# The context's first chunk in full fp32 between the products of the lead, in both FFNs of a trunk layer

## The chip, the cores and the metric

The kernel runs on one core of a Trainium2 chip. The metric is the device time of one execution in microseconds, the lower the better. TensorE has two clock levels here, 1.2 and 2.4 GHz; the profile gives the granted clock as a share of the higher one.

## The reference

One layer of a flow-matching backbone for 128 context tokens and 1024 latent tokens (1152 rows of 1024 features), everything in fp32:

```python
def _swiglu(h, w1, w2):
    a, b = jnp.split(h @ w1, 2, axis=-1)
    return (jax.nn.silu(a) * b) @ w2

def _layer(x, mod, lw, rope, kv_ctx):
    f1 = _swiglu(_modulate(x, sh1, sc1), lw['ffn1_w1'], lw['ffn1_w2'])
    x = _layer_norm(ALPHA * x + 0.5 * g1 * f1, ...)
    mix, k, v = _mixer(_modulate(x, sh2, sc2), lw, rope, kv_ctx)
    x = _layer_norm(ALPHA * x + g2 * mix, ...)
    f2 = _swiglu(_modulate(x, sh3, sc3), lw['ffn2_w1'], lw['ffn2_w2'])
    x = _layer_norm(ALPHA * x + 0.5 * g3 * f2, ...)
```

`w1` of an FFN is 1024 x 5632 and `w2` 2816 x 1024. The modulation is x * (1 + scale) + shift per feature, with one pair of vectors for the context and one for the latents.

## The kernel before

**Products.** A matrix product in near-fp32 accuracy is made of three fp32r matmuls (`mm3`, L130 to L132). Each operand is split into a high part, rounded by ScalarE (an ACTIVATE with Copy, L107), and the rest, subtracted on VectorE (L108). TensorE also takes plain fp32 operands: the trace then shows two records for one matmul. The transposes (L135), the modulation's products (L224) and the context's attention scores (L1348) are such plain fp32 work.

**An FFN.** The latent rows are 1024, in two halves of 512. The first weight matrix is worked through in 22 pairs of blocks of 128 columns. A pair is computed by a scheme with seven products in place of eight, on the halves of rows, features and columns: `A11`, `A12`, `S1`, `S2`, `S4`, `S3`, `A22`, in this order. Their moving operands, the two halves of x and sums and differences of them, are split once per FFN; the weights, sums of them too, are split for each pair. The first four pairs are the **lead** (`lead`): they run product by product, all four pairs through one product before the next, so that the operands can be made meanwhile. The text calls A11 the lead's first product, A12 its second, S1 its third and S2 its fourth. `up` then runs the other 18 pairs one behind another, and `down` the second matrix.

In the lead, `first_sum` loads two blocks of a pair's weights and subtracts them (L711) into the third product's weight; for the fourth, L738 subtracts once more. `second` adds the second product's bank into SBUF (L667), which frees the bank. There are eight PSUM banks of 128 x 512; four hold `Y` of the four pairs for most of the lead.

In the first FFN, x comes from the inputs already transposed, and the modulation vectors themselves are computed during the lead (`mod_head`). In the second (`begun`), the first product runs at the end of the mixer (`lead_first`), and the pieces of x are loaded from DRAM, transposed on TensorE and modulated on ScalarE (L402, `piece_dram`): first-half pieces (`piece(0, k)`) and second-half pieces (`piece(1, k)`). `S1` needs the second half only.

**The context.** Its 128 rows go through both FFNs on their own (`ctx_ffn`), in six chunks of columns: five of 512 per half of w1, one of 256. A chunk takes eight weight tiles of 128 x 1024 (`w1c`, 512 KB), each with two output banks; then silu, product, transposes, and the rows of `w2`. `ctx_ffn` is a generator that yields after each piece of work, 155 in all. `tick(n)` advances it n times, and the calls of `tick` in `lead` and `up_prod` set where its work stands in the program. Before, the first FFN gives it to the side queue behind the lead; the second FFN advances it 18 times in the lead ahead of the third product's weights (that is the first chunk) and 5 times in the last product.

**Buffers and queues.** Weight tiles from DRAM go through a ring of five buffers (`raw`, 128 x 1024), loaded on SP's queue. Rings `pc`, `tmp`, `b2`, `xm`, `ts` hold pieces, sums and operands. The program is traced in this order and then planned by the framework with modelled times (`schedule_with_timeline_sim=True`): an instruction traced earlier has priority, and one whose operands and buffers are there may go ahead of it. The engines then run the planned order strictly, waiting on semaphores.

Of the kernel before, what the change touches and what calls it, by code (L numbers as in the profile page):

```python
# [32 lines left out]
P = 128  # L33
# [21 lines left out]
class Layer:  # L55
# [364 lines left out]
    def piece_dram(self, n, kc):  # L420
        r = self.raw(self.x2_d[1 + n][:, :, kc * P : (kc + 1) * P], 512)
        b = self.bank()
        for t in range(4):
            self.transpose(b[:, t * P : (t + 1) * P], r[:, t * P : (t + 1) * P])
        m = self.piece_place(n, kc)
        self.modulated(m, b, 2, LAT, kc)
        return m
# [6 lines left out]
    def open_early(self, right):  # L434
# [7 lines left out]
        def gen():  # L442
            for kc in range(KC):
                self.first_operand(self.piece_dram, kc)
                yield
            yield from self.ctx_x_dram()
# [29 lines left out]
    def ctx_operands(self):  # L476
        place = self.xm if "xm" in self.pools else self.pc
        self.xc = [(place(F32R), place(F32R)) for _ in range(2)]

    def ctx_x(self, x, i, kcs):  # L480
        for kc in kcs:
            m = self.pc()[:, :P]
            self.modulated(m, x[kc], i, CTX, kc)
            ks = slice(kc % 4 * P, (kc % 4 + 1) * P)
            self.split(self.xc[kc // 4][0][:, ks], self.xc[kc // 4][1][:, ks], m)

    def ctx_x_dram(self):
        self.ctx_operands()
        for h in range(2):
            m = self.raw(self.x2_d[0][:, h * 512 : (h + 1) * 512], 512)  # L490
            b = self.bank()
            js = [slice(j * P, (j + 1) * P) for j in range(4)]
            for j in js:
                self.transpose(b[:, j], m[:, j])
            for k, j in enumerate(js):
                self.modulated(m[:, j], b[:, j], 2, CTX, 4 * h + k)
            self.split(self.xc[h][0], self.xc[h][1], m)
            yield

    def ctx_up(self, b, w, kc, n):  # L500
        hi, lo = self.wide(self.raw(w, 2 * n), 2 * n)
        ks = slice(kc % 4 * P, (kc % 4 + 1) * P)
# [6 lines left out]
    def ctx_ffn(self, i, x, w1c, w1t, w2):  # L509
        nc = self.nc  # L510
        if x:
            self.ctx_operands()
            x()
        yield
        acc = None
        for c in range(6):
            n = 256 if c == 5 else 512
            banks = [self.bank(), self.bank()]
            for kc in range(KC):
                yield from self.ctx_up(banks, w1t[kc] if c == 5 else w1c[c, kc], kc, n)  # L520
            h = self.tmp() if c == 0 and "xm" in self.pools else self.pc()
# [58 lines left out]
    def up_pair(self, m, w1, h_d):  # L580
# [17 lines left out]
        self.up_prod(Z, "A12", (hi[:, 512:], lo[:, 512:]), True, 1 + self.spare * (m < 15))  # L598
# [12 lines left out]
        self.up_prod(Y, "S2", [halves(w)[1] for w in t12], False, 1 + self.spare)  # L611
# [38 lines left out]
    def lead(self, w1, h_d, piece, make, Y=None):  # L650
# [44 lines left out]
        else:  # L695
# [6 lines left out]
            self.tick(18)  # L702
# [10 lines left out]
        if begun:  # L713
            for p in R:
                first_sum(p)
            W = [self.wide(T[p], 512) for p in R]
            self.first = [piece(0, k) for k in R]
# [12 lines left out]
        else:  # L730
            for p in R:
                first_sum(p)
                X.append(self.bank())
                prod(X[p], "S1", self.wide(T[p], 512), True)
# [15 lines left out]
        for p in R:  # L750
# [11 lines left out]
            if begun and p == 0:  # L762
# [223 lines left out]
    def ffn(self, i, head, res_of, dst, order, half, beside=None, begun=None):  # L986
# [3 lines left out]
        with ExitStack() as st:  # L990
# [13 lines left out]
            if begun:  # L1004
                self.add_side(context)
            self.lead(a["w1_" + s], h_d, piece, make, Y)
            self.mods = mods
            if not begun:
                self.add_side(context)
# [12 lines left out]
    def head_input(self):  # L1022
        nc, a = self.nc, self.a

        def ctx_x():
            for q in range(4):
                x = self.pc()
                nc.sync.dma_start(x[:, :256], a["x_c"][q])
                self.ctx_x({q: x[:, :P], q + 4: x[:, P:256]}, 0, (q, q + 4))
# [17 lines left out]
        return self.piece_input, make, ctx_x, mods()  # L1047

    def head_dram(self):
        return self.piece_dram, lambda kc: None, None, self.mod_part(8)  # L1050
# [536 lines left out]
def _layout(inputs):  # L1587
# [32 lines left out]
    for i, w in enumerate(WINDOWS):  # L1620
# [6 lines left out]
        "x_c": con(x[:P].T.reshape(2, 4, P, P).transpose(1, 2, 0, 3)).reshape(4, P, 256),  # L1627
# [56 lines left out]
```

## Time and profile before

| | |
|---|---|
| time, median of 3 runs | 2495.24 us (2494.67 to 2498.43) |
| the profiled execution's own time | 2495.49 us |
| its span, first to last instruction | 2493.7 us |
| mean granted TensorE clock | 0.995 |
| busy: TensorE, VectorE, ScalarE | 2452.3, 1830.6, 1214.5 us |

A matmul's record has the time from its start to its modelled end. Matmuls overlap, so the pace is read from the starts, and a bracket behind a row gives the idle time before it and what ended it. PE is TensorE, DVE is VectorE, ACT is ScalarE, POOL is GpSimd, SP issues DMAs; PEq, SPq and so on are their queues.

### The profile page before, as it was taken

How to read it: one execution, taken by the hardware profiler on the slowest of the kernel's cores; microseconds unless marked ns; L12 is line 12 of the kernel's file. 1: busy time of each engine (PE TensorE's matmuls, PEld its weight loads, DVE VectorE, ACT ScalarE, POOL GpSimd, SP SyncE). 2: the span in 40 equal slices, each digit the busy share in tenths (PEclk: the TensorE clock that was granted, in tenths of full speed). 3: DMA queues.
4: the chain of work that ended last, by engine and by line, in shares of the span. 5: the costliest groups of instructions: out<-in, count | busy, mean ns of one | idle time of the engine just before them, and what ended most of it. 6: DMA issues, size and time to landing. Idle time of an engine off the chain costs nothing.

```text
span 2493.7 us, 34226 instructions
## 1 busy us (share of the span) xinstructions
PE 2452.3 (98%) x12297; PEld 2115.0 (85%) x12297; DVE 1830.6 (73%) x2817; ACT 1214.5 (49%) x2094; POOL 463.4 (19%) x691
## 2 busy tenths in 40 slices
PE   8999999999999999999999999999899999999998
PEld 4788888888889989889999999998688888887887
DVE  6877778877678556566888886876877666676877
ACT  5544444444445343434778773435744344444442
POOL 0000011110022212232567640110000001111002
PEclk9999999999999999999999999999999999999999
DMA  7455566778686555534100035665754445558773
GB/s 292 144 167 188 182 224 230 244 259 326 213 276 218 184 180 189 188 136 163 42 1 2 1 110 187 237 215 185 223 173 164 150 173 195 205 197 320 269 267 121
DMA packets 167554, 463.75 MB, mean 186 GB/s; under 512 B 18900, under 2 KB 37636, under 8 KB 167384
## 3 DMA queue, kind: packets, MB, share of 16 engines
q1 hardware_dynamic: 140952, 373.79, 44.7%
q0 software_dynamic: 23696, 86.32, 9.3%
q8 instruction: 97, 1.59, 0.3%
q10 hardware_dynamic: 2736, 1.44, 0.2%
q14 instruction: 73, 0.60, 0.1%
HBM read 390.42 MB, written 71.07 MB: 185 GB/s over the span
## 4 chain that ended last, share of the span: by engine, by line
PE 84%; DVE 6%; issue 4%; DMA 3%; ACT 2%; POOL 1%; SPq 0%; DVEq 0%; POOLq 0%; ACTq 0%
PE w L130 24%; PE w L131 24%; PE w L132 24%; PE w L1060 8%; PE w L135 3%; DVE op L108 1%; DVE x L108 1%; DMA raw<-w 1%; DVE mx L1389 1%; PE w L224 0%; DMA yc<-fc 0%; ACT pr L1397 0%; DMA raw<-w1c 0%; DVE so L108 0%; DMA raw<-x 0%
## 5 line engine op out<-in xcount | busy, mean ns | idle before, releaser
L107 ACT ACTIVATE op<-raw 128x1024 fp32r<-128x1024 f32 (+1 forms) x505 | 483.9, 969 | 517.4 <-PE w L131 263.4
L108 DVE TENSOR_TENSOR op<-raw,op 128x1024 fp32r<-128x1024 f32 (+1 forms) x505 | 558.9, 1116 | 233.1 <-ACT op L107 201.1
L130 PE MATMUL w<-b,op 128*128 128x512 f32 x880 | 343.9, 393 | 7.1 <-ACT b L107 2.9
L131 PE MATMUL w<-b,op 128*128 128x512 f32 x880 | 344.6, 392 | 0.0
L132 PE MATMUL w<-b,op 128*128 128x512 f32 x880 | 339.7, 391 | 0.3 <-DVE op L108 0.3
L130 PE MATMUL w<-x,op 128*128 128x384 f32 x768 | 260.0, 339 | 0.0
L131 PE MATMUL w<-x,op 128*128 128x384 f32 x768 | 258.8, 337 | 0.0
L132 PE MATMUL w<-x,op 128*128 128x384 f32 x768 | 257.7, 337 | 0.0
L131 PE MATMUL w<-op,so 128*128 128x512 f32 (+1 forms) x627 | 242.4, 387 | 2.0 <-DVE op L108 2.0
L132 PE MATMUL w<-op,so 128*128 128x512 f32 (+1 forms) x627 | 241.9, 387 | 0.0
L130 PE MATMUL w<-op,so 128*128 128x512 f32 (+1 forms) x627 | 232.7, 386 | 1.0 <-ACT op L107 0.9
L130 PEld LDWEIGHTS w<-b,op 128*128 128x128 f32 x880 | 165.6, 188 | 42.9 <-ACT b L107 3.4
L562 POOL DMA_DIRECT2D h<-tmp x80 | 43.4, 543 | 851.6 <-DVE tmp L626 426.1
L132 PEld LDWEIGHTS w<-b,op 128*128 128x128 f32 x880 | 165.8, 188 | 35.8 <-DVE op L108 0.8
L131 PEld LDWEIGHTS w<-b,op 128*128 128x128 f32 x880 | 165.8, 188 | 34.8 <-DVE b L108 0.7
L1402 POOL TENSOR_TENSOR pr<-pr,sm 128x384 f32<-128x384 f32 x192 | 156.1, 842 | 95.1 <-DVE sm L1400 71.8
L190 DVE SCALAR_TENSOR_TENSOR junk<-raw,sil 128x1024 bf16<-128x1024 f32 x112 | 135.9, 1224 | 26.0 <-DMA raw<-w_mod 25.6
L107 ACT ACTIVATE so<-sr 128x1024 fp32r<-128x1024 f32 (+1 forms) x84 | 82.7, 986 | 136.1 <-PE w L131 82.7
L131 PEld LDWEIGHTS w<-x,op 128*128 128x128 f32 x768 | 144.1, 188 | 0.3
L130 PEld LDWEIGHTS w<-x,op 128*128 128x128 f32 x768 | 144.1, 188 | 0.4
L132 PEld LDWEIGHTS w<-x,op 128*128 128x128 f32 x768 | 143.9, 188 | 0.0
L131 PEld LDWEIGHTS w<-op,so 128*128 128x128 f32 x627 | 118.2, 189 | 26.8 <-DVE op L108 3.2
(323 smaller groups left out, 5136.6 us busy)
## 6 DMA issues: line engine op xcount, KB each, us to landing
raw<-w SPq DMA_DIRECT2D x240, 256.0 KB, 5.3
raw<-w SPq DMA_DIRECT2D x116, 512.0 KB, 3.9
raw<-w1c SPq DMA_DIRECT2D x80, 512.0 KB, 4.0
sr<-h SPq DMA_DIRECT2D x70, 512.0 KB, 5.7
raw<-w_mod SPq DMA_DIRECT2D x56, 512.0 KB, 4.3
raw<-w_gate SPq DMA_DIRECT2D x48, 512.0 KB, 3.7
h<-tmp POOLq DMA_DIRECT2D x80, 256.0 KB, 3.6
h<-pc POOLq DMA_DIRECT2D x52, 256.0 KB, 4.6
```

The source lines that it names most:

```text
L107: self.nc.scalar.activation(hi, src, AF.Copy)
L108: self.nc.vector.tensor_tensor(lo, src, hi.bitcast(F32), ALU.subtract)
L130: mm(out, lhsT=lh, rhs=rh, start=start, stop=False)
L131: mm(out, lhsT=lh, rhs=rl, start=False, stop=False)
L132: mm(out, lhsT=ll, rhs=rh, start=False, stop=stop)
L135: self.nc.tensor.transpose(out, src, self.ident)
L190: nc.vector.scalar_tensor_tensor(junk, w, 1.0, self.sil[cond], ALU.mult, ALU.mult, accum_out=self.mod[:, cond, b : b + 1],)
L562: self.nc.gpsimd.dma_start(h_d[f // 2][:, 2 * kh + n, f % 2, :], h)
L1060: self.nc.tensor.matmul(acc[h][j], lhsT=lhs[:, part, js], rhs=w[wi][:, h * 512 : (h + 1) * 512], start=f, stop=l)
L1389: nc.vector.tensor_reduce(mx[:, c : c + 1], b[:, :GT], AX.X, ALU.max)
L1402: nc.gpsimd.tensor_tensor(pr[:, c, :], pr[:, c, :], sm[:, 3:4].broadcast_to([P, GT]), ALU.mult)
```

## The change

In both FFNs the context's first chunk is computed with one plain fp32 matmul per weight tile and bank, on modulated rows (`xf`) and weights that are not split. The rows of the first FFN are loaded in two tiles and modulated in place; they are loaded, modulated and split again for the other chunks (`ctx_parts_input`, at the second chunk). Those of the second FFN are modulated at the end of the mixer as before, and split at the second chunk (`ctx_parts_dram`).

The first FFN's context now joins the side queue ahead of the lead, and both leads make the 18 calls behind the third product's weights (loads, sums and splits of all four pairs) and ahead of its matmuls, and the 5 calls in the last product. The calls in `up_prod` of the first FFN are fewer by the same number. In the second FFN the raw loads of the second-half pieces go through POOL's queue into slots of `b2` instead of the ring of five.

```diff
     def piece_dram(self, n, kc):
-        r = self.raw(self.x2_d[1 + n][:, :, kc * P : (kc + 1) * P], 512)
+        src = self.x2_d[1 + n][:, :, kc * P : (kc + 1) * P]
+        if n == 0:
+            r = self.raw(src, 512)
+        else:
+            r = self.pools["b2"].tile([P, 512], F32, tag="b2", name=self.name("xr"), bufs=12)
+            self.nc.gpsimd.dma_start(r.rearrange("p (a b) -> p a b", a=4), src)
...
-            yield from self.ctx_x_dram()
+            yield from self.ctx_whole_dram()
...
-    def ctx_x(self, x, i, kcs):
-        for kc in kcs:
-            m = self.pc()[:, :P]
-            self.modulated(m, x[kc], i, CTX, kc)
-            ks = slice(kc % 4 * P, (kc % 4 + 1) * P)
-            self.split(self.xc[kc // 4][0][:, ks], self.xc[kc // 4][1][:, ks], m)
...
+    def ctx_whole_input(self):
+        self.xf = [self.tmp() for _ in range(2)]
+        for h, x in enumerate(self.xf):
+            self.nc.sync.dma_start(x, self.a["x_c"][h])
+            for k in range(4):
+                js, kc = slice(k * P, (k + 1) * P), 4 * h + k
+                self.modulated(x[:, js], x[:, js], 0, CTX, kc)
+
+    def ctx_parts_input(self):
+        self.xc = [(self.pc(F32R), self.pc(F32R)) for _ in range(2)]
         for h in range(2):
-            m = self.raw(self.x2_d[0][:, h * 512 : (h + 1) * 512], 512)
+            m = self.pc()
+            self.nc.sync.dma_start(m, self.a["x_c"][h])
+            for k in range(4):
+                js = slice(k * P, (k + 1) * P)
+                self.modulated(m[:, js], m[:, js], 0, CTX, 4 * h + k)
+            self.split(self.xc[h][0], self.xc[h][1], m)
+
+    def ctx_whole_dram(self):
+        self.xf = []
+        for h in range(2):
+            r = self.raw(self.x2_d[0][:, h * 512 : (h + 1) * 512], 512)
             b = self.bank()
+            x = self.xm()
+            self.xf.append(x)
             js = [slice(j * P, (j + 1) * P) for j in range(4)]
             for j in js:
-                self.transpose(b[:, j], m[:, j])
+                self.transpose(b[:, j], r[:, j])
             for k, j in enumerate(js):
-                self.modulated(m[:, j], b[:, j], 2, CTX, 4 * h + k)
-            self.split(self.xc[h][0], self.xc[h][1], m)
+                self.modulated(x[:, j], b[:, j], 2, CTX, 4 * h + k)
             yield
 
-    def ctx_up(self, b, w, kc, n):
+    def ctx_parts_dram(self):
+        self.xc = []
+        for x in self.xf:
+            hi, lo = self.xm(F32R), self.pc(F32R)
+            self.split(hi, lo, x)
+            self.xc.append((hi, lo))
+
+    def ctx_up(self, b, w, kc, n, whole):
+        ks = slice(kc % 4 * P, (kc % 4 + 1) * P)
+        if whole:
+            r = self.raw(w, 2 * n)
+            for s in range(2):
+                self.nc.tensor.matmul(
+                    b[s][:, :n], lhsT=self.xf[kc // 4][:, ks], rhs=r[:, s * n : (s + 1) * n],
+                    start=kc == 0, stop=kc == KC - 1,
+                )
+                yield
+            return
         hi, lo = self.wide(self.raw(w, 2 * n), 2 * n)
...
+        whole, parts = x
+        if whole:
+            whole()
         yield
         acc = None
         for c in range(6):
             n = 256 if c == 5 else 512
             banks = [self.bank(), self.bank()]
+            if c == 1:
+                parts()
             for kc in range(KC):
-                yield from self.ctx_up(banks, w1t[kc] if c == 5 else w1c[c, kc], kc, n)
-            h = self.tmp() if c == 0 and "xm" in self.pools else self.pc()
+                yield from self.ctx_up(banks, w1t[kc] if c == 5 else w1c[c, kc], kc, n, c == 0)
+            h = self.tmp() if c == 0 else self.pc()
...
-        self.up_prod(Z, "A12", (hi[:, 512:], lo[:, 512:]), True, 1 + self.spare * (m < 15))
+        self.up_prod(Z, "A12", (hi[:, 512:], lo[:, 512:]), True, 1 + self.spare * (m < 10))
...
-        self.up_prod(Y, "S2", [halves(w)[1] for w in t12], False, 1 + self.spare)
+        self.up_prod(Y, "S2", [halves(w)[1] for w in t12], False)
...
             for p in R:
                 second(p, self.bank(), True)
-            self.tick(18)
...
             W = [self.wide(T[p], 512) for p in R]
+            self.tick(18)
             self.first = [piece(0, k) for k in R]
...
         else:
             for p in R:
                 first_sum(p)
+            W = [self.wide(T[p], 512) for p in R]
+            self.tick(18)
+            for p in R:
                 X.append(self.bank())
-                prod(X[p], "S1", self.wide(T[p], 512), True)
+                prod(X[p], "S1", W[p], True)
                 self.next_operand(p, *S[p])
...
-            if begun and p == 0:
+            if p == 0:
                 self.tick(5)
...
-            if begun:
-                self.add_side(context)
+            self.add_side(context)
             self.lead(a["w1_" + s], h_d, piece, make, Y)
             self.mods = mods
-            if not begun:
-                self.add_side(context)
```

The context's input is laid out as two tiles of 128 x 512 to suit.

## Rows read from the trace of the kernel before

**Rows 1.** The page's busy times: us, share of the span, instructions.
```profile
PE 2452.3 (98%) x12297; PEld 2115.0 (85%) x12297; DVE 1830.6 (73%) x2817; ACT 1214.5 (49%) x2094; POOL 463.4 (19%) x691
```
**Rows 2.** Busy time by stretch: length, engines, granted clock, DMA share, GB/s.
```profile
47.00:72.00 25.00, 19.18 (x70) 13.48 (x68) 24.81 (x49) 19.25 (x35) 0.00 (x0) 0.86 0.27 83
72.00:1757.00 1685.00, 1671.87 (x8865) 1492.49 (x8864) 1247.78 (x2027) 848.31 (x1592) 390.48 (x576) 1.00 0.52 175
1757.00:1800.00 43.00, 35.66 (x176) 26.83 (x175) 31.42 (x45) 28.67 (x43) 0.66 (x2) 1.00 0.71 216
65.00:70.00 5.00, 4.48 (x11) 3.52 (x12) 5.00 (x9) 4.40 (x8) 0.00 (x0) 0.50 0.36 103
```
**Rows 3.** TensorE in order of time, first lead: start, duration, line.
```profile
60.02 0.39 PE L132 MATMUL w<-ax,op 128*128 128x512 f32 x1
...
65.52 0.79 PE L130 MATMUL w<-b,op 128*128 128x512 f32 x1 [2.52 <-DVE tmp L667]
...
70.33 0.40 PE L132 MATMUL w<-b,op 128*128 128x512 f32 x1
```
**Rows 4.** VectorE in order of time, both leads.
```profile
60.56 0.69 DVE L738 TENSOR_TENSOR ts<-raw,ts 128x512 f32<-128x512 f32 x1
...
64.78 2.48 DVE L667 TENSOR_TENSOR tmp<-w,tmp 128x512 f32<-128x512 f32 x4
...
1758.89 1.22 DVE L108 TENSOR_TENSOR op<-raw,op 128x1024 fp32r<-128x1024 f32 x1
```
**Rows 5.** Waits of TensorE, 1757 to 1800: total us, times, longest.
```profile
PE w L135 <- DMA raw<-x: 3.0, 5, 1.5
PE w L130 <- ACT b L107: 2.9, 2, 2.3
PE w L135 <- ACT xp L402: 0.8, 2, 0.6
PE w L132 <- DVE op L108: 0.3, 1, 0.3
```
**Rows 6.** TensorE in order of time: fp32 matmuls and what starts next.
```profile
29.28 3.62 PE L224 MATMUL w<-wm,silt 128*2 128x256 f32 x16
32.83 1.20 PE L130 MATMUL w<-ax,op 128*128 128x512 f32 x4
...
1185.93 1.05 PE L1348 MATMUL w<-kcT,q 128*128 128x128 f32 x8
1186.74 0.42 PE L131 MATMUL w<-x,op 128*128 128x384 f32 x1
```
**Rows 7.** TensorE in order of time: first and last of 26 fp32r matmuls.
```profile
73.08 0.39 PE L130 MATMUL w<-b,op 128*128 128x512 f32 x1
...
78.74 0.39 PE L131 MATMUL w<-b,op 128*128 128x512 f32 x1
```
**Rows 8.** ScalarE's groups by form, 0 to 130: busy us, mean ns.
```profile
L107 ACT ACTIVATE op<-raw 128x1024 fp32r<-128x1024 f32 x5 | 5.2, 1059 | 6.6 <-PE w L131 4.5 <-PE w L132 2.1
...
L402 ACT ACTIVATE pc<-pc,md 128x128 f32<-128x128 f32 x8 | 3.8, 488 | 3.9 <-DMA pc<-x_c 3.9
```
**Rows 9.** Waits of SP's queue, 1757 to 1800.
```profile
SPq L111 <- PE w L135: 15.8, 12, 3.1
```
**Rows 10.** POOL in order of time, second lead.
```profile
1821.66 0.55 POOL L562 DMA_DIRECT2D h<-tmp  x1 [62.39 <-DVE tmp L748]
```
**Rows 11.** DMA of 1766 to 1786: packets, MB, share; size, us to landing.
```profile
q1 hardware_dynamic: 8491, 4.77, 83.1%
...
raw<-x SPq DMA_DIRECT2D x16, 256.0 KB, 3.6
```
**Rows 12.** TensorE in order of time, second lead: chunk, transposes, third product.
```profile
1757.57 0.40 PE L130 MATMUL w<-op,xm 128*128 128x512 f32 x1
...
1775.01 0.63 PE L135 MATMUL w<-ident,raw 128*128 128x128 f32 x4 [0.78 <-DMA raw<-x]
...
1778.73 0.73 PE L130 MATMUL w<-b,op 128*128 128x512 f32 x2 [2.25 <-ACT b L107]
```

More of the change, by code (lines that the diff above doesn't have):

```diff
@@ L473, in last_operands @@
         self.A["A22"].append(self.parted(r, "b2", 12))
-    def ctx_operands(self):
-        place = self.xm if "xm" in self.pools else self.pc
-        self.xc = [(place(F32R), place(F32R)) for _ in range(2)]
-    def ctx_x(self, x, i, kcs):
-        for kc in kcs:
-            m = self.pc()[:, :P]
-            self.modulated(m, x[kc], i, CTX, kc)
-            ks = slice(kc % 4 * P, (kc % 4 + 1) * P)
-            self.split(self.xc[kc // 4][0][:, ks], self.xc[kc // 4][1][:, ks], m)
-    def ctx_x_dram(self):
-        self.ctx_operands()
-        for h in range(2):
-            m = self.raw(self.x2_d[0][:, h * 512 : (h + 1) * 512], 512)
+    def ctx_whole_input(self):
[5 more added lines that the diff above has]
+                self.modulated(x[:, js], x[:, js], 0, CTX, kc)
@@ L501, in ctx_up @@
         hi, lo = self.wide(self.raw(w, 2 * n), 2 * n)
-        ks = slice(kc % 4 * P, (kc % 4 + 1) * P)
         xh, xl = self.xc[kc // 4]
@@ L510, in ctx_ffn @@
         nc = self.nc
-        if x:
-            self.ctx_operands()
-            x()
+        whole, parts = x
+        if whole:
+            whole()
         yield
@@ L1023, in head_input @@
         nc, a = self.nc, self.a
[L1025 to L1029, printed above, removed]
         def mods():
@@ L1045, in make @@
                 self.spread(1, rows[2:])
-        return self.piece_input, make, ctx_x, mods()
+        return self.piece_input, make, (self.ctx_whole_input, self.ctx_parts_input), mods()
     def head_dram(self):
-        return self.piece_dram, lambda kc: None, None, self.mod_part(8)
+        return self.piece_dram, lambda kc: None, (None, self.ctx_parts_dram), self.mod_part(8)
     def x2_of(self, t):
@@ L1626, in _layout @@
         "x_l": con(x[P:].T.reshape(KC, P, 2, 512).transpose(2, 0, 1, 3)[::-1]),
-        "x_c": con(x[:P].T.reshape(2, 4, P, P).transpose(1, 2, 0, 3)).reshape(4, P, 256),
+        "x_c": con(x[:P].T.reshape(2, 4, P, P).transpose(0, 2, 1, 3)).reshape(2, P, 512),
         "w_mod": con(wm_t[16:]),
```

## The prediction

> **What bounds the kernel.** I read the page's busy times first: TensorE is busy 98% of the span [rows 1]. So a microsecond comes off only where TensorE waits or runs at the lower clock, and every column added to it elsewhere is paid in full. Next I took stretches. From 72 to 1757 us, from the end of the first FFN's lead to the middle of the second's, TensorE waits 13 us in 1685. The change touches two stretches outside it, 47 to 72 and 1757 to 1800, with 5.8 and 7.3 us of idle time [rows 2].
>
> Then TensorE's own order in time, with what ended each wait. In the first lead it is done with the second product at 60.4 and makes a real start only at 65.52, behind a wait for the additions that empty the second product's banks (L667) [rows 3]. From 65 to 70 the granted clock is 0.50, the lower level [rows 2]; at 70.33 the matmuls are back at their full pace. Between 60.4 and 70.3 it ran 13 matmuls (11 of them from 65 on), worth 13 x 0.226 = 2.9 us; the other 7.0 us are what this place costs. VectorE has no idle time there, and the additions stand at 64.78 in its queue, behind seven pieces of work for later products that it began after 60.4 [rows 4]. In the second lead the named waits are for the loads of x (3.0 us), for splits (2.9 and 0.3) and for the modulation (0.8) [rows 5].
>
> **The added columns.** The chunk's three fp32r matmuls per bank and k-tile become one fp32 matmul. The trace has fp32 matmuls already. In the modulation's products (L224) 8 matmuls of 256 columns make 16 records, and the next instruction starts 3.55 us after the first: 1.73 ns a column, 0.887 us for 512. Of those with 128 columns (L1348) four make eight records and take 0.81 us [rows 6]. Three fp32r matmuls of 512 take 0.68: 26 of them begin 0.226 us apart [rows 7]. I take 0.887, since L224 is nearer in width: 0.207 us more, 32 times (2 FFNs, 8 k-tiles, 2 banks), **+6.6 us**. The ends: 32 x (0.81 - 0.68) = 4.2, and, if one fp32 matmul costs as much as four fp32r, 32 x 0.226 = 7.2.
>
> **What the splits free.** Each of 16 weight tiles loses an ACTIVATE of 1.06 us [rows 8] and a subtraction of 1.22 [rows 4]: 17 us of ScalarE and 20 of VectorE, by themselves worth nothing, since TensorE hardly waits for either outside the two stretches [rows 2]. What counts is that a chunk of 16 x 0.887 = 14.2 us can run while both catch up.
>
> **First lead.** The chunk is now issued after the third product's four weights and ahead of its matmuls. But it needs two PSUM banks. The lead holds four of the eight for Y, and the other four are those that L667 empties. So it can start no sooner than the third product could. Only what stands ahead of L667 on VectorE decides. Two of those pieces are the sums for the fourth product's weights (L738, 0.60 us apart) [rows 4]; their loads now queue behind the chunk's eight tiles in a ring of five buffers, so they go later: **-1.2 us**. The rest (operands of later products) has its inputs either way, and I leave it where it is. An idle time over 3 us stays, and with it the lower clock. Nothing gained, and all 7.0, are the ends. After 72 TensorE does not wait in this lead before either, so the slack that the chunk gives VectorE has nothing more to save.
>
> ScalarE gets the chunk's eight modulations here, 8 x 0.488 = 3.9 us [rows 8]. Before, they came in the later products of the lead. Where ScalarE waits for VectorE they cost nothing; ahead of the last operand's split they would delay all that follows by up to 3.9. I take 0, since that split is issued before them. The second modulation and the splits at the second chunk, and the context's second load (0.5 MB), fall where TensorE does not wait [rows 2]. So do the moved calls (one extra per pair up to pair 9 instead of 14, and one less in each fourth product): the number of pieces is the same and none is late.
>
> **Second lead.** Here the chunk already stood between the products; its columns are counted above. Two things move. The third product's weights are loaded, subtracted and split ahead of the chunk. And the second half of x no longer waits for one of the five buffers: SP's queue spends 15.8 us of this stretch waiting for transposes to free one [rows 9]. The new loads stand on POOL's queue and go to free slots. They must wait for the last rows of x to be written. POOL issues that store until 1759.3 and is then idle for 62 us, so nothing is held up behind them [rows 10]. With the 3.6 us that a load takes to land [rows 11], put for the store, that is 1763 for the first. During x's loads the queue moves 4.77 MB in 20 us at 83% use [rows 11], 0.287 MB a microsecond when full: eight loads of 0.26 MB take 7.3 us. So the first lands before 1767 and the eighth at 1774 or earlier; the chunk ends at 1757.6 + 14.2 = 1771.8 [rows 12]. On SP the last three tiles of the chunk now wait for TensorE itself to free a buffer, one every 1.8 us; behind them wait the first half of x and the fourth product's weights, not needed for the 11 us of the third product (16 x 0.68).
>
> So the 3.0 us for loads go. What is late next is the chain from a transpose through modulation, sum and split to the first matmul: 1775.01 to 1778.73, 3.7 us [rows 12]. Four groups of transposes (0.45 each) cover 1.8 of it and 1.9 stays. The smaller waits, for modulation (0.8) and for splits behind the first (0.65 and 0.3) [rows 5], I leave: 1.7. Of 7.3 us 3.6 stay, **-3.7 us**. The ends: 0 and -7.3.
>
> **Sum.** 6.6 - 1.2 - 3.7 = +1.7 us on the profiled execution's 2495.49: 2497.2. The median of the runs is 0.25 below that execution, so **2496.9 us**. A change of under 0.2%, 5.0 us, can't be told from none on this kernel.
>
> **Rivals.**
>
> *Slower: the loads of x still set the second lead's pace.* Place: 1763 to 1780. For it: the one queue already takes 83% of the 16 DMA engines' time there [rows 11], and the chunk's last tiles (1.5 MB) now fall into the same time. Against: only half of x is wanted first. If that half lands as late as it was transposed before, past 1775, the 3.7 us are not regained: 6.6 - 1.2 = +5.4, 2500.6 us. The Trainium skill, page "Trainium Kernel Development and Optimization", section Key Constraints, says that DMAs of the SP, ACT and POOL queues run on the same 16 engines, and that several issuers save only issue time. By that rule the new queue buys nothing and this rival holds; the trace agrees that the engines are nearly full, but it shows SP waiting for buffers, of which the rule does not speak.
>
> *The first lead closes wholly.* If L667 comes up on VectorE right behind the second product's end, TensorE goes on at 61, the clock holds, and all 7.0 come back: 6.6 - 7.0 - 3.7 = -4.1, 2491.1 us. For it: nothing in the data holds L667 past 60.5. Against: VectorE's order is planned beforehand, and the plan up to there sees the same inputs.
>
> *Transposes run inside the second lead's chunk*, since two banks are free and x is there: all 7.3 come back, 6.6 - 1.2 - 7.3 = -1.9, 2493.3 us. With the rival before it: -7.7, 2487.5 us.
>
> *The chunk does not run where it is issued.* If the planned order puts it behind the third product, the first lead keeps its 7.0 and the columns stay: 6.6 - 3.7 = +2.9, 2498.1 us, which I count with the forecast.
>
> **Chances.** Forecast 0.42, slower rival 0.25, first lead alone 0.10, transposes alone 0.08, both 0.15. Faster by over 0.2% is the case of both and half of the first lead's: 0.20. Slower is most of the slower rival, and a little of the forecast whose gains fail: 0.25. Within: 0.55. The range leaves out half of the case of both, and the little past the worst end (7.2 and nothing regained, 2502.4): 2488 to 2502. The forecast's own, with each gain halved or half again as large, is 2494 to 2499.5.
>
> **What would show it.** The chunks' matmuls: 64 records, 0.43 to 0.45 us apart, and no split of their tiles. First lead: L667 near 63.5, TensorE idle some 3 us before the chunk, the lower clock when it begins. Second lead: no wait for x's loads, one wait of about 2 us behind the chunk. I am wrong if an fp32 column costs other than 1.73 ns, if TensorE waits within a chunk for its weights, or if a new wait stands behind one.

## The result and the profile after

| | before | after |
|---|---|---|
| time, median of 6 runs each | 2495.26 us (2494.67 to 2498.43) | 2512.51 us (2508.06 to 2514.47) |
| the profiled execution, its span | 2495.49, 2493.7 us | 2508.06, 2506.0 us |

The ratio is 1.0065, 95% interval 1.0052 to 1.0078: 16 us slower, outside the predicted range. The profiled execution of after is the fastest of its six, 12.6 us above that of before and 4.5 under the median of its own kernel; what follows is read from it. After the change L698 is the addition that was L667, L772 the fourth product's weight sum that was L738, L462 and L467 the operand sums that were L457 and L462, and L525 the fp32 matmul.

Two marks cut the trace at places that every version passes: the first gating of the residual behind the mixer (L339), which starts when the second FFN's lead is about to begin, and the last store of the lead's h. First before, then after, from VectorE's and POOL's order in time:

```profile
1733.78 2.48 DVE L339 TENSOR_TENSOR ry<-w,gate 128x512 f32<-128x512 f32 x4
```

```profile
1850.37 0.54 POOL L562 DMA_DIRECT2D h<-pc  x1 [2.18 <-DVE pc L760]
```

```profile
1731.67 2.48 DVE L339 TENSOR_TENSOR ry<-w,gate 128x512 f32<-128x512 f32 x4
```

```profile
1862.90 0.54 POOL L593 DMA_DIRECT2D h<-pc  x1 [4.99 <-DVE pc L794]
```

The stretch between the marks (below: the second lead) grew from 116.6 to 131.2 us, **+14.6**. Up to the first mark the kernel is 2.1 us ahead; behind the second it needs 643.3 and 643.1 us. So all of the loss of this execution is in the second lead. The stretches after, for [rows 2], with 60 to 65 besides:

```profile
47.00:72.00 25.00, 20.88 (x65) 12.38 (x66) 24.82 (x46) 21.17 (x40) 0.00 (x0) 0.93 0.43 155
72.00:1757.00 1685.00, 1672.62 (x8853) 1490.40 (x8852) 1236.73 (x2012) 837.22 (x1576) 389.27 (x575) 1.00 0.51 175
1757.00:1800.00 43.00, 27.94 (x103) 17.45 (x102) 15.60 (x24) 16.14 (x26) 7.38 (x11) 0.84 0.58 177
60.00:65.00 5.00, 3.76 (x5) 1.71 (x6) 5.00 (x9) 2.69 (x5) 0.00 (x0) 0.66 0.01 3
65.00:70.00 5.00, 5.00 (x13) 2.29 (x12) 5.00 (x9) 4.06 (x8) 0.00 (x0) 1.00 0.13 45
```

In 1757 to 1800 TensorE is busy 27.9 us of 43 where it was 35.7, and the clock fell to 0.84. TensorE's waits there, for [rows 5]:

```profile
PE w L135 <- DMA raw<-x: 6.9, 2, 3.7
PE w L130 <- ACT b L107: 6.6, 1, 6.6
```

TensorE's own order in that place, for [rows 12]: the chunk is done at 1769.46, two tiles of x are transposed, the third and fourth come late, and the third product starts at 1787.69 instead of 1778.73.

```profile
1755.44 14.18 PE L525 MATMUL w<-raw,xm 128*128 128x512 f32 x32
1769.46 1.38 PE L135 MATMUL w<-ident,raw 128*128 128x128 f32 x8
1774.03 0.63 PE L135 MATMUL w<-ident,raw 128*128 128x128 f32 x4 [3.19 <-DMA raw<-x]
1778.32 1.09 PE L135 MATMUL w<-ident,raw 128*128 128x128 f32 x4 [3.66 <-DMA raw<-x]
...
1787.69 1.22 PE L130 MATMUL w<-b,op 128*128 128x512 f32 x2 [6.57 <-ACT b L107]
```

The chain of waits says what came before that start (start, duration, piece):

```profile
1767.94 10.25 DMA raw<-x
...
1778.32 1.10 PE w L135 x4
...
1779.44 2.93 DMA raw<-w
...
1782.40 0.70 DVE ts L772
...
1785.68 0.70 DVE ts L772
```

A load of the first half of x takes 10.25 us to land; only behind its transpose are the ring's buffers free for the fourth product's weights; VectorE stands at the sum of these weights (L772), and behind it at the next, before it comes to the first sum of the third product's operands (L462):

```profile
1782.40 0.69 DVE L772 TENSOR_TENSOR ts<-raw,ts 128x512 f32<-128x512 f32 x1 [11.98 <-DMA raw<-w]
...
1785.68 0.69 DVE L772 TENSOR_TENSOR ts<-raw,ts 128x512 f32<-128x512 f32 x1 [1.21 <-DMA raw<-w]
1786.29 0.68 DVE L462 TENSOR_TENSOR pc<-pc,pc 128x512 f32<-128x512 f32 x1
...
1792.31 0.69 DVE L772 TENSOR_TENSOR ts<-raw,ts 128x512 f32<-128x512 f32 x1 [0.49 <-DMA raw<-w]
1792.92 0.69 DVE L462 TENSOR_TENSOR pc<-pc,pc 128x512 f32<-128x512 f32 x1
```

All four weight sums stand ahead of the second operand sum. Before, the first operand sum came at 1777.32 and the first weight sum (L738) at 1788.76, behind all four operand sums:

```profile
1777.32 0.69 DVE L457 TENSOR_TENSOR pc<-pc,pc 128x512 f32<-128x512 f32 x1 [3.71 <-ACT pc L402]
...
1788.76 0.69 DVE L738 TENSOR_TENSOR ts<-raw,ts 128x512 f32<-128x512 f32 x1 [1.10 <-DMA raw<-w]
```

The DMA of 1766 to 1786, for [rows 11]: both queues together take 86% of the 16 engines, and the median load of x on SP's queue, of those whose landing the profile tells, needs 9.6 us where it needed 3.6.

```profile
q1 hardware_dynamic: 4553, 2.72, 49.8%
q0 software_dynamic: 640, 2.10, 36.6%
...
xr<-x POOLq DMA_DIRECT2D x6, 256.0 KB, 7.5
raw<-x SPq DMA_DIRECT2D x6, 256.0 KB, 9.6
```

In the first lead (VectorE, then TensorE, for [rows 3, 4]) the addition stands at 60.44 instead of 64.78, and the chunk starts at 61.24:

```profile
60.44 0.69 DVE L698 TENSOR_TENSOR tmp<-w,tmp 128x512 f32<-128x512 f32 x1
```

```profile
61.24 5.27 PE L525 MATMUL w<-raw,tmp 128*128 128x512 f32 x8 [2.75 <-ACT b L107]
```

### The profile page after: what moved, and what is told of

It is laid out like the page before. It is cut to its first block, busy times and chain, and to the rows that moved or that the text cites. A ratio compares the mean times of both kernels' runs of the same rounds, so it can differ in the third digit from the quotient of the medians.

```text
span 2506.0 us, 34117 instructions
## 1 busy us (share of the span) xinstructions
PE 2455.7 (98%) x12265; PEld 2109.8 (84%) x12265; DVE 1812.8 (72%) x2795; ACT 1200.8 (48%) x2080; POOL 468.0 (19%) x699
## 4 chain that ended last, share of the span: by engine, by line
PE 87%; DVE 6%; DMA 3%; ACT 2%; issue 1%; POOL 0%; SPq 0%; DVEq 0%; POOLq 0%; ACTq 0%
PE w L130 25%; PE w L131 25%; PE w L132 25%; PE w L1085 8%; PE w L135 3%; DMA raw<-w 2%; DVE op L108 1%; PE w L525 1%; DVE x L108 1%; DVE mx L1414 1%; ACT pr L1422 0%; PE w L224 0%; DMA yc<-fc 0%; DMA raw<-x 0%; DMA raw<-w_mod 0%
## 5 line engine op out<-in xcount | busy, mean ns | idle before, releaser
L107 ACT ACTIVATE op<-raw 128x1024 fp32r<-128x1024 f32 (+1 forms) x489 | 466.4, 966 | 525.8 <-PE w L131 269.8
L108 DVE TENSOR_TENSOR op<-raw,op 128x1024 fp32r<-128x1024 f32 (+1 forms) x489 | 539.9, 1114 | 230.2 <-ACT op L107 192.2
L131 PEld LDWEIGHTS w<-b,op 128*128 128x128 f32 x880 | 165.7, 188 | 36.6 <-DVE b L108 2.1
```

The lines of the kernel that those rows point to most:

```text
L107: self.nc.scalar.activation(hi, src, AF.Copy)
L108: self.nc.vector.tensor_tensor(lo, src, hi.bitcast(F32), ALU.subtract)
L131: mm(out, lhsT=lh, rhs=rl, start=False, stop=False)
```

## The experiments

Three suspects stood at the start, A: the second half's loads on POOL's queue, by shared DMA engines or by the planned order that they bring; B: the fp32 chunk, which holds the ring's buffers at TensorE's pace; C: the third product's weights ahead of the chunk. All sixteen kernels, with the second lead's length by the marks in the profiled execution. There is one profile of each:

| kernel | median us | ratio to before, 95% | second lead us |
|---|---|---|---|
| before | 2494.8 to 2495.5 | 1 | 116.6 |
| the change | 2512.51 | 1.0052 to 1.0078 | 131.2 |
| first FFN only | 2496.61 | 0.9995 to 1.0014 | 116.5 |
| loads on SP | 2497.24 | 0.9999 to 1.0018 | 119.1 |
| second chunk split | 2511.44 | 1.0047 to 1.0077 | 132.2 |
| weights behind | 2517.12 | 1.007 to 1.01 | 140.1 |
| queue alone | 2515.46 | 1.0067 to 1.0093 | 139.7 |
| sums in order | 2495.64 | 0.9995 to 1.0014 | 116.7 |
| order alone | 2500.22 | 1.0017 to 1.0035 | 123.9 |
| in order, second chunk split | 2501.72 | 1.0017 to 1.0039 | 123.8 |
| in order, first chunk split | 2505.47 | 1.0034 to 1.0057 | 123.9 |
| the same, loads on SP | 2504.08 | 1.0026 to 1.0057 | 120.7 |
| in order, both split | 2509.23 | 1.0049 to 1.0075 | 128.1 |
| first half late | 2505.84 | 1.0026 to 1.0055 | 127.2 |
| the same, loads on SP | 2503.45 | 1.0022 to 1.0048 | 126.6 |
| the same, sums in order | 2506.28 | 1.003 to 1.0055 | 127.2 |
| second half first | 2504.85 | 1.0028 to 1.0053 | 127.1 |
| the same, loads on SP | 2501.65 | 1.0019 to 1.0037 | 124.2 |

Behind the second mark most kernels need 642.4 to 643.3 us. Four need less, since some of the work that follows runs ahead of their last store (behind it TensorE has 2806 to 2813 matmul records instead of 2821 to 2826): in order with the second chunk split 638.7, in order with both split 638.9, queue alone 639.6, order alone 641.3. Their second leads are longer by that much, 2 to 4 us, without a loss of time.

**First FFN only.** The second FFN is wholly as before. Its other hunks, the split chunk and the place of the 18 calls, are those shown below under "Second chunk split" and "Weights behind".

```diff
-        if n == 0:
-            r = self.raw(src, 512)
-        else:
-            r = self.pools["b2"].tile([P, 512], F32, tag="b2", name=self.name("xr"), bufs=12)
-            self.nc.gpsimd.dma_start(r.rearrange("p (a b) -> p a b", a=4), src)
+        r = self.raw(src, 512)
...
-            yield from self.ctx_whole_dram()
+            yield from self.ctx_split_dram()
...
```

> Only the first FFN is changed; the second FFN's lead is the old one (chunk split, ahead of the weights, all of x through the ring on SP). From the traces the first FFN ends 2.1 us earlier than before and the second lead takes 14.6 us longer. If the two add up and the loss is all in the second lead: 2493.2 us, 2 below the kernel before. If the first lead's gain needs nothing else but something later pays for it: 2495 or more.

1.0005: the first FFN's part costs -1.2 to +3.5 us. The loss is the second FFN's.

**Loads on SP.** Of the whole change only the second half's loads go back to SP's queue and the ring (the first hunk above).

> Everything as in the changed kernel, but the second half of x is loaded again on SP's queue through the ring of five. Theory A (the loads on POOL's queue are the cause: they share the DMA engines with the first half's loads, which TensorE takes first, and they change the planned order, so that VectorE and ScalarE wait for the fourth product's weights ahead of the third product's operands): most of the 14.6 us come back, 2494 to 2499 us. Theory B (the chunk in fp32 holds the ring until TensorE is through with each tile, so that x's loads come late): no better than the changed kernel, 2508 or more, since now both halves wait for the ring. Theory C (third product's weights ahead of the chunk): unchanged, 2508 to 2512.

1.0008: nearly all 16 us are gone with the queue, and the fp32 chunk and the moved weights stay. The operand sums are first again on VectorE, the weight sums (L768) behind them:

```profile
1778.51 0.69 DVE L458 TENSOR_TENSOR pc<-pc,pc 128x512 f32<-128x512 f32 x1 [4.90 <-ACT pc L402]
...
1791.34 0.69 DVE L768 TENSOR_TENSOR ts<-raw,ts 128x512 f32<-128x512 f32 x1 [1.51 <-DMA raw<-w]
```

**Second chunk split.** The second FFN's first chunk in three fp32r matmuls as before; POOL's loads and the moved weights stay.

```diff
-            yield from self.ctx_whole_dram()
+            yield from self.ctx_split_dram()
...
-                yield from self.ctx_up(banks, w1t[kc] if c == 5 else w1c[c, kc], kc, n, c == 0)
+                yield from self.ctx_up(banks, w1t[kc] if c == 5 else w1c[c, kc], kc, n, c == 0 and i == 0)
```

> Everything as in the changed kernel, but the second FFN's first chunk is split into fp32r again (loads on POOL and weights ahead of the chunk stay). Theory A: the loss stays but for the 3 us of added columns, 2505 to 2510 us. Theory B: the loss goes, 2493 to 2497. Theory C: as A.

2511.44: the fp32 chunk is not the cause. B falls. It is a little over what A expected, since the 3 us of columns did not come back.

**Weights behind.** The 18 calls stand ahead of the third product's weights again, in the second FFN.

```diff
             for p in R:
                 second(p, self.bank(), True)
+            self.tick(18)
...
             W = [self.wide(T[p], 512) for p in R]
-            self.tick(18)
```

> Everything as in the changed kernel, but in the second lead the 18 calls stand ahead of the third product's weights again (fp32 chunk and loads on POOL stay). Theory A: the loss stays, 2505 to 2512 us. Theory B: it stays. Theory C: most of it goes, 2494 to 2499.

2517.12, 4.6 us slower than the change and 5 over what A expected: C falls too, and the moved weights help as long as the rest is late.

**Queue alone.** The second FFN as before but for one edit, which changes two things at once: the queue of the second half's loads, and the slots of `b2` that they land in instead of the ring of five.

> First FFN as in the change; in the second, everything as in the kernel before (chunk in three fp32r matmuls, 18 pieces of the context ahead of the third product's weights), except that the second-half loads of x go through POOL's queue into slots of b2. If the queue of these loads alone turns the planned order on VectorE (in the plan of this kernel two of the fourth product's sums do stand ahead of the third product's first operand sum), this single edit costs about what the change does: 2510 to 2517 us, with TensorE waiting over 10 us for loads of x and splits behind the chunk, at a clock under 0.8 in 1775 to 1790. If it takes the edit together with the fp32 chunk or the moved weights, it is near the first-FFN-only kernel: 2496.6 us.

2515.46 against 2496.61 with the first FFN only, as expected by A: this one edit brings the whole loss. Whether the queue or the slots do it was not tested apart. TensorE waits 6.8 us for x and 8.7 for the operands' split, and VectorE has two weight sums ahead of the first operand sum:

```profile
1779.11 3.75 PE L135 MATMUL w<-ident,raw 128*128 128x128 f32 x16 [6.77 <-DMA raw<-x]
...
1792.96 1.22 PE L130 MATMUL w<-b,op 128*128 128x512 f32 x2 [8.74 <-ACT b L107]
```

```profile
1787.57 0.69 DVE L781 TENSOR_TENSOR ts<-raw,ts 128x512 f32<-128x512 f32 x1 [5.29 <-DMA raw<-w]
...
1791.56 0.68 DVE L462 TENSOR_TENSOR pc<-pc,pc 128x512 f32<-128x512 f32 x1
```

**Sums in order.** The change, with the fourth product's weight sums held on VectorE behind the third product's four operand sums. The loads stay on POOL's queue.

```diff
-        tt(s, s, r, ALU.add)
+        self.last_sum = tt(s, s, r, ALU.add).ins
...
             r = part(1, p, 1)
-            sub(T[p], r, T[p])
+            if begun:
+                with self.tc.issue_after(self.last_sum):
+                    sub(T[p], r, T[p])
+            else:
+                sub(T[p], r, T[p])
```

> Everything as in the changed kernel, but VectorE's sums for the fourth product's weights are held behind the four sums for the third product's operands (the first half's transposes still come first on TensorE, loads on POOL). This parts the two halves of the order: if the weights' place on VectorE and ScalarE is most of it, 2498 to 2502 us; if it is the first half's transposes waiting for loads that share the engines with POOL's, 2504 to 2510.

2495.64, under both of the ranges expected: 17 us come back, and the second lead is as long as before. VectorE's order:

```profile
1778.67 0.69 DVE L462 TENSOR_TENSOR pc<-pc,pc 128x512 f32<-128x512 f32 x1 [5.00 <-ACT pc L402]
...
1788.32 0.69 DVE L774 TENSOR_TENSOR ts<-raw,ts 128x512 f32<-128x512 f32 x1
```

By itself this would put the whole loss on the order. The next runs show that it isn't all.

**Order alone.** Loads on SP, and the first half of the wrong order made by hand: two weight sums are traced ahead of the operand sums, which are held behind them. Nothing of x goes through POOL's queue. In the change the other two weight sums come before the second operand sum; here they come behind all four. The edit also puts the loads of its two weights ahead of the last four loads of x on SP's queue.

```diff
+            halves1 = [(piece(1, k), piece(1, k + 4)) for k in R]
+            for p in range(2):
+                r = part(1, p, 1)
+                early = sub(T[p], r, T[p]).ins
             for k in R:
-                S.append(self.sum_operands(piece, k))
+                with self.tc.issue_after(early):
+                    S.append(self.sum_operands(piece, k, halves1[k]))
...
-            r = part(1, p, 1)
-            sub(T[p], r, T[p])
+            if not (begun and p < 2):
+                r = part(1, p, 1)
+                sub(T[p], r, T[p])
```

> The change with all loads of x on SP's queue (2497.2 us, sums in the old order), but with the third product's four operand sums held on VectorE behind the fourth product's first two weight sums. No second queue takes part. If the order is the cause, the first operand sum moves from 1778.5 to some 1787 to 1791, when the fourth product's weights have landed (in the run it starts from, its first weight sum is at 1791.3): 8 to 13 us more, 2505 to 2510 us. If the sharing of the DMA engines by the two queues is the cause, it stays at 2497.2.

2500.22, 3.0 us over the loads on SP: less than the 8 to 13 expected. The second lead is 4.8 longer, and 1.9 of it is made good behind the mark. The operand sums come at 1785.86 instead of 1778.51, but then all four run in a row:

```profile
1784.04 0.69 DVE L749 TENSOR_TENSOR ts<-raw,ts 128x512 f32<-128x512 f32 x1 [10.06 <-DMA raw<-w]
1785.25 0.69 DVE L749 TENSOR_TENSOR ts<-raw,ts 128x512 f32<-128x512 f32 x1 [0.52 <-DMA raw<-w]
1785.86 2.49 DVE L458 TENSOR_TENSOR pc<-pc,pc 128x512 f32<-128x512 f32 x4
```

**In order, one or both chunks split.** From the sums in order, the first FFN's chunk, the second's (as above), or both in three fp32r matmuls; and the first of these with loads on SP.

```diff
-                yield from self.ctx_up(banks, w1t[kc] if c == 5 else w1c[c, kc], kc, n, c == 0)
+                yield from self.ctx_up(banks, w1t[kc] if c == 5 else w1c[c, kc], kc, n, c == 0 and i == 1)
...
-        return self.piece_input, make, (self.ctx_whole_input, self.ctx_parts_input), mods()
+        return self.piece_input, make, (self.ctx_parts_input, lambda: None), mods()
```

> The kernel with the fourth product's sums held behind the third's operands (2495.6 us), with the first FFN's first chunk in three fp32r matmuls at the new place between the products. If the fp32 chunk only adds columns there: 2495.6 - 3.1 = 2492.5 us. If it is needed since VectorE has no idle time in that stretch, eight subtractions of 1.22 us (9.8 us) stand ahead of the later products' operands or the tiles' splits wait behind them: up to 9.8 - 3.1 = 6.7 us more, 2495.6 to 2502.3 us, with TensorE waiting for splits of w1c tiles within the chunk.

> The kernel with the fourth product's sums held behind the third's operands (2495.6 us), with the second FFN's first chunk in three fp32r matmuls again. If the fp32 chunk only adds columns there, the second chunk gives back 16 x (0.876 - 0.68) = 3.1 us: 2492.5 us. If its freedom from splits is what lets VectorE and ScalarE finish the third product's operands in time, TensorE waits for weight splits within the chunk or behind it, and the time stays or rises: 2495.6 to 2500 us.

> Both first chunks in three fp32r matmuls, the rest as in the kernel with the fourth product's sums held behind the third's operands (2495.6 us). If the two fp32 chunks only add columns: 2495.6 - 6.3 = 2489.3 us, faster than the kernel before (2495.1). If the fp32 chunk is what makes room on VectorE and ScalarE in each lead: 2496 to 2507 us.

> The kernel with the first FFN's chunk in three fp32r matmuls and the sums in order (2505.5 us, of which some 7 us were lost in the second lead, whose planned order is that of the 2495.6 us kernel), with the second-half loads of x back on SP's queue. If two queues sharing the DMA engines cost those 7 us, the second lead falls to what it takes with loads on SP, about 2.5 us over before: 2505.5 - 4.7 = 2500.8 us. If the sharing is not the reason: 2505.5.

All are slower than the sums in order, by 6 to 14 us, though 3.1 or 6.3 us of columns are gone; the three with POOL's loads are over every range expected. With the first chunk split, the first lead waits again (waits of 50 to 100 us):

```profile
PE w L130 <- DVE tmp L698: 4.0, 1, 4.0
PE w L131 <- DVE op L108: 3.8, 3, 1.3
```

The second lead of that kernel has the same order of instructions as the sums in order on every engine, and is 7.2 us longer. What differs is when things landed. POOL's order in time and the store's time to landing, first with the sums in order, then with the first chunk split too:

```profile
1762.22 0.60 POOL L350 DMA_DIRECT2D x<-ry  x1 [1.62 <-DVE ry L349]
1771.01 5.96 POOL L426 DMA_DIRECT2D xr<-x  x8 [8.19 <-DMA raw<-w1c]
```

```profile
x<-ry POOLq DMA_DIRECT2D x1, 512.0 KB, 8.1
```

```profile
1763.88 0.60 POOL L350 DMA_DIRECT2D x<-ry  x1 [1.62 <-DVE ry L349]
1767.81 5.24 POOL L426 DMA_DIRECT2D xr<-x  x7 [3.33 <-DMA x<-ry]
```

```profile
x<-ry POOLq DMA_DIRECT2D x1, 512.0 KB, 3.3
```

POOL's loads wait for the store of x's last rows. With the sums in order the store, issued at 1762.22, took 8.1 us, until about 1770.3 (the row names a weight load that ended about then), and these loads began at 1771.01, 7.3 us behind SP's first-half loads (from 1763.75). With the first chunk split it took 3.3, and the loads began at 1767.81, 0.4 us behind SP's (from 1767.37). Then TensorE waits 5.0 us for the first half:

```profile
1780.96 1.09 PE L135 MATMUL w<-ident,raw 128*128 128x128 f32 x4 [5.03 <-DMA raw<-x]
...
1788.34 0.93 PE L130 MATMUL w<-b,op 128*128 128x512 f32 x2 [2.48 <-ACT b L107]
```

With loads on SP and all else the same, the second lead is 120.7 us: in this pair of profiles the sharing cost 3.2. The expected 4.7 on the time came out as 1.4, which the two intervals do not tell from none. In the two profiles the spans are equal: the first FFN, the same program in both, took 2.9 us longer with the loads on SP (mark at 1738.46 against 1735.58).

**First half later.** Five kernels let the first half of x wait: traced behind the third pair of the third product (with POOL's loads, with loads on SP, with the sums in order), or four pieces of it between the second and third pair (with the sums in order, on POOL and on SP).

```diff
-            self.first = [piece(0, k) for k in R]
...
                 if p == 2:
-                    self.first += [piece(0, 4 + k) for k in R]
+                    self.first = [piece(0, k) for k in range(8)]
```

For the second half first, the first of these lines moves behind the loop over the third product's first two pairs, and the other stays.

> Everything as in the changed kernel, loads on POOL too, but the pieces of the first half of x are traced behind the third product (only the fourth needs them). Now the second half's transposes come first on TensorE and VectorE's sums for the third product stand ahead of the fourth's weights. If the planned order is what costs (first half's transposes and the fourth product's weights in front of the third product's operands): nearly all comes back, 2490 to 2497 us. If sharing the DMA engines costs by itself: the loads are as many in the same time, and 2500 to 2508 stay.

> As the run before it, but the second half of x is loaded on SP's queue through the ring of five. If the ring is what the chunk's tiles and x fight for, this is slower than with POOL's queue: 2496 to 2500 us. If only the order counts, the same as with POOL within 1 us.

> Both edits of the order together (first half behind the third product, fourth product's sums behind the third's operands), loads on POOL. If each half of the order has its own cost, this is the fastest of the four: 2489 to 2495 us. If the first edit alone already sets the order right, the same as it within 1 us.

> The kernel with the sums in order (2495.6 us), with the first-half pieces of x traced behind the third product's first two pairs, so that TensorE transposes the second half first; the loads' queues are as before. If the first half's landing holds the third product, its start comes up to 3 us earlier: 2492.5 us. If POOL's loads are the later ones (they wait for the store of x, and in the kernel it starts from they began at 1771.0), it waits for them and for banks: 2495.6 to 2503 us.

> The same with all loads of x on SP's queue, the second half first in it. One queue, nothing shared, and the half that is wanted first comes first: the first operand sum at some 1775 instead of 1778.5, so 2497.2 - 3.5 = 2493.7 us, if the first half's transposes can run between the third product's pairs. If they wait for banks and modulations there, as in the runs with the first half late (3.5 us and more), 2497 to 2503 us.

None gains: they are 7 to 11 us over before. Three came out in the less hopeful of the two cases expected: the first half late, the same with the sums in order, and the second half first on SP; the other two in neither. The first of the five starts its operand sums in time, but TensorE then waits four times for a bank that a modulation must empty (3.5 us in all), and the first weight sum comes at 1799.30, 11 us later than with the sums in order:

```profile
1777.58 0.69 DVE L462 TENSOR_TENSOR pc<-pc,pc 128x512 f32<-128x512 f32 x1 [3.50 <-ACT pc L402]
...
1799.30 0.69 DVE L771 TENSOR_TENSOR ts<-raw,ts 128x512 f32<-128x512 f32 x1 [0.77 <-DMA raw<-w]
```

## Why the prediction was wrong

**The step that failed** is "So the 3.0 us for loads go", the -3.7 us of the second lead, with what it leaned on: that the first half of x and the fourth product's weights are "not needed for the 11 us of the third product". The forecast for the second lead was 3.3 - 3.7 = -0.4 us; it cost +14.6. With that in its place, the forecast would be 2511.9 against 2512.51. That they are so close is in part luck: the 14.6 is read from an execution 4.5 us under the median.

Both are needed, by the order in which the engines run. On TensorE the four first-half pieces stand ahead of the second half; the code says so (`self.first = [piece(0, k) for k in R]` ahead of the sums), and I looked only at which data the third product uses. On VectorE the plan of the changed kernel puts two weight sums ahead of the first operand sum and the other two ahead of the second. Weight sums came ahead of operand sums in every kernel with the loads on POOL's queue, the first half in its place and no order forced, whichever of the fp32 chunk and the moved weights was taken out (with the second chunk split one stands ahead of the first operand sum, in the others two). They did not in the kernels with these loads on SP's queue, the first half in its place and none forced. Why the planner's modelled times turn it, by the queue or by the slots that free the ring, was not looked into.

**Sizes.** Loads on SP: +2.5 us over before, about the added columns, so nothing is regained even there; TensorE's wait for loads of x is down from 3.0 to 0.4 us in that kernel (1735 to 1830), but one of 1.3 for the chunk's own tiles has come, and one of 1.2 for modulations. On top of that the second lead grows by 4.8 with the order made by hand (3.0 on the time), by 3.2 (pair with the first chunk split) to 4.8 (against the loads on SP) with the two queues, and by 12.1 with the change. Each is a difference of two single profiles, and in the fourteen profiles with the change's first FFN the first mark alone varies by 3.5 us. So the parts are estimates, and that they add up to less than the change is not explained: the order made by hand is only half of the change's, and in the change the weights that VectorE waits for are themselves late. What is shown is that the edit of the loads brings the loss, and that holding VectorE's order takes it back while the loads stay on POOL's queue; how the loss divides between order and sharing stays open.

The sums in order escaped both: the order by the edit, the sharing, as far as its one profile shows, because the store landed late. Its ten runs all lie between 2494.3 and 2499.3, so what helps it recurs; whether the store lands late in each of them is not known. Its median, 2495.64, is within 1.3 us of the forecast 2496.9, but by landing times that the forecast did not have.

**The landing times.** I put the first of POOL's loads at 1763 (it was issued at 1764.31) and the eighth's landing at 1774 or earlier, from eight loads alone on the engines. Issued until 1770.84 and landing in a median 7.2 us, the last is there at about 1778. The first half on SP shares the engines in the same time.

**The slower rival** named the right direction and a part of the mechanism, the loads of x on shared engines, with the price of a gain not made (+5.4 us in all). Both halves of x were wanted at once, and it had no thought of the planned order; so its price was 12 us too small. The Trainium skill, page "Trainium Kernel Development and Optimization", section Key Constraints, has the DMAs of SP, ACT and POOL queues on the same 16 engines and interleaving. The runs agree: in 1766 to 1786 the two queues take 49.8 and 36.6% where one took 83.1, little more together, and SP's loads land in 9.6 us instead of 3.6. Which load is slowed matters: the fourth load of the first half, which stands ahead of all of the second on TensorE, took 10.25 us in the change and 4.5 with the sums in order, issued at 1771.19, where TensorE waited 1.7 us for it. I had set the rule against SP's waits for buffers and should have priced both.

**The added columns** were right: the second chunk's 16 matmuls are 32 records in 14.02 us, 0.876 us each for the 0.887 predicted, 32 x (0.876 - 0.68) = +6.3 us.

**The first lead** was right in kind and small in size. L698 came at 60.44 where I expected L667's place near 63.5; the chunk starts behind an idle 2.75 us (predicted 3). The lower clock came, as predicted, but earlier: 0.66 in 60 to 65, and 1.00 in 65 to 70, where before had 0.50. Over the fourteen profiles with this first FFN the first mark lies between 1731.67 and 1735.12, mean 1733.8, and that of before in its one profile is the same: by this the 3.1 us of added columns are regained up to there, not 1.2. The rival that the lead closes wholly did not come, nor the one with transposes inside the second chunk: the first begins at 1769.46, behind it. Of the first chunk's 32 records 20 run ahead of the third product and 12 between its matmuls, a part of the last rival.

**What the splits free.** "By themselves worth nothing" holds away from the leads. In the first lead, splitting the chunk again cost 6.8 us (loads on SP: 2504.08 against 2497.24; the second lead is 1.6 of it) although 3.1 us of columns went. The first mark is later in all three pairs that differ in this chunk, by 4.2, 1.8 and 5.2 us: there the fp32 chunk pays for itself. For the second lead it is not settled: with the sums in order, the chunk split again cost 6.1 us, but its POOL loads also began 1.8 us behind SP's, so that sharing is in that number, and its profile, the fastest of its six runs, is only 1.7 us over.

No version beat the kernel before; the sums in order are level with it.

## What to carry to other kernels

A load that is moved to another queue changes more than its own wait: ask which loads it will run beside, and which of them the engines come to first in their order. Where a planner orders the engines, read the new order at the place of the change before counting any gain there; an operation with priority by place and no inputs yet can stand ahead of the one that is wanted. A kernel may be fast because a store landed late, as one profile here suggests: compare two versions with the same planned order before crediting an edit.

## What the runs showed of the hardware

- Two queues that loaded x at once stretched a 256 KB load's landing from 3.6 us to 9.6 on SP's queue and took 7.2 to 7.5 on POOL's. With the queue alone, SP's first four loads of x, issued from 1766.35 to 1772.19 among POOL's, took 9.4 to 12.7 us by their semaphores; the other four, issued from 1780.25 when POOL's had landed, took 3.2 to 4.7.
- The 512 KB store of x landed 3.3 us after it was issued in one kernel and 8.1 in another with the same order of instructions there; their second leads differ by 7 us, of which 3.2 went when x was loaded on SP's queue alone.
- Around the stalls the granted clock sank below full: 0.73 in 1770 to 1780 and 0.67 in 1780 to 1790 after the change, where TensorE was busy 3.0 and 3.4 us of ten (columns as in [rows 2]). With the queue alone the first of these was 0.50, the lower level all through.

```profile
1770.00:1780.00 10.00, 2.99 (x17) 2.55 (x17) 0.42 (x1) 2.88 (x4) 0.75 (x1) 0.73 1.09 288
1780.00:1790.00 10.00, 3.43 (x15) 2.73 (x14) 5.26 (x8) 3.62 (x7) 0.00 (x0) 0.67 0.28 94
```
